# Mixing x before its context in layer 0 of a two-stream block, with the split weights kept in DRAM

## The chip, the cores and the metric

One core of a Trainium2 chip runs one program. Its engines are TensorE (PE, with the load of the stationary operand shown as PEld), VectorE (DVE), ScalarE (ACT), GpSimd (POOL) and SyncE (SP), which issues nearly all DMAs. The metric is the device time of one execution in microseconds. A profile of one execution is shown beside the runs' times; its rows and lines are those of the kernel's source.

## The reference

All tensors are float32. Block 1 has two layers over two streams, x of 512 tokens and a context of 256, both 1024 wide, with the same weights. What concerns the change is the mixer of layer 0, which both streams go through:

```python
for l in range(DEPTH):                       # DEPTH = 2
    h  = modulate(rms_norm(x,  mix_pre_g[l]), sh1,  sc1)
    hc = modulate(rms_norm(xc, mix_pre_g[l]), shc1, scc1)
    p, pc = h @ w_in[l], hc @ w_in[l]        # last layer: only k, v of pc
    # q, k, v; k_all = [kc, k], v_all = [vc, v]
    attn = latent_attention(q, k_all, v_all)
    y = mixer_merge(p, attn, w_attn_o[l], ..., w_gmlp_o[l], ..., w_conv_o[l], w_out[l])
    x = x + g1 * rms_norm(y, mix_post_g[l])
    h2 = modulate(rms_norm(x, ffn_pre_g[l]), sh2, sc2)
    x = x + g2 * rms_norm(square(relu(h2 @ w_ff1[l])) @ w_ff2[l], ffn_post_g[l])
    if not last:                             # the same for the context, on kc, vc alone
        yc = mixer_merge(pc, gqa_attend(qc, kc, vc), ...)
        xc = xc + gc1 * rms_norm(yc, ...)
        xc = xc + gc2 * rms_norm(feed forward of hc2, ...)

def mixer_merge(...):
    a_out = attn @ w_attn_o
    g_out = chunk_spatial_gate(gelu(gu), rms_norm(gelu(gv)), ws, bs) @ w_gmlp_o
    c_out = silu(layer_norm(conv31(a * sigmoid(b)))) @ w_conv_o
    return (ga * a_out + gg * g_out + gc * c_out) @ w_out
```

The context of layer 0 takes keys and values of its own only; those of x take the context's too. A second block of other mixers follows, which the change leaves as it is.

## The kernel before, in words

Activations lie by feature: a tensor of 1024 features is eight tiles of 128 rows, with its tokens along the free axis (`FM`). Every large product is made in three parts. Each operand is given as two float32r parts, hi and lo, whose sum is the float32 value, and `mm3` (L219) multiplies hi by hi, hi by lo and lo by hi. A weight comes in chunks of 128 x 1024 (512 KB), which make one tile of 128 output features; `gemm` (L226) gives 24 products for it, of 256 columns for the context and 512 for x.

`wload` (L195) brings a chunk: a DMA into a tile wr, a cast on ScalarE that gives wh, and a subtraction that gives wl, on VectorE or, if `pool_share` is 2, on GpSimd for every second chunk. There are four slots each of wr, wh and wl. The wr slots are shared with the chunks of `ada_w` (L396), from which background jobs make the modulation vectors.

```python
nc.sync.dma_start(raw, ap)
nc.scalar.copy(hi, raw)
eng.tensor_tensor(lo, raw, hi.bitcast(F32), ALU.subtract)
```

`first_block` (L954) sets the order. In layer 0: four column groups of `ada_w`; the context's norm, K and V; the context's `mixer` (L824) with `pool_share` at 2 and its w_out, beside which x is normed; K and V of x, in two halves of 256 tokens; the `mixer` of x, with the rest of layer 0's `ada_w` beside it and the rest of the context's mixer (`chain_jobs`: residual, norm, feed-forward input) at its end; w_out of x in halves; then the feed-forward `ff` (L859) of both streams.

A mixer has the attention (`attention`, L503), the branch of `w_attn_o`, the spatial gate (`gmlp`), the branch of `w_gmlp_o`, and at the end the branch of `w_conv_o`. Beside the first branches run the 31 taps of the convolution for each of eight tiles (`conv_jobs`, L692, taps at L722), as background jobs spread over about 45 units of products; `conv_act_jobs` then norms the result beside the eight gates of the last branch. 88 chunks of 512 KB are used by each mixer (queries 8, convolution inputs 16, gates 24, three output projections 24, gu 8, gv 8), and w_out has 8 more.

`ff` computes the hidden layer in quarters. The first quarter has two passes over the same eight chunks, back and forth: the context and the first half of x, then the second half of x, since the chain of that half runs beside the first pass.

The framework schedules the whole program: it fixes each engine's order ahead of the run from a timeline that it computes. On each engine, instructions are taken up in that order.

Of the kernel before, what the change touches and what calls it, by code (L numbers as in the profile page):

```python
# [17 lines left out]
P = 128  # L18
D = 1024
# [18 lines left out]
class FM:  # L38
    """A [n * 128, T] tensor kept as tiles of 128 rows, two to a slot if T is 256."""
# [15 lines left out]
class Cols:  # L55
    """Columns c0..c1 of an FM."""
# [20 lines left out]
class Parts:  # L77
    """An FM in parts of 256 tokens that live on their own."""
# [15 lines left out]
def advance(g, n=1):  # L94
    """Up to n steps of a generator; False when it is done."""
    for _ in range(n):
        if next(g, "end") == "end":
            return False
    return True


def interleave(a, b, na, nb):
    """na steps of a, then nb of b, and so on until both are done."""
    la = lb = True
    while la or lb:
        la = la and advance(a, na)
        lb = lb and advance(b, nb)


class Builder:  # L110
    def __init__(self, es, tc, I):
        self.tc, self.nc, self.I = tc, tc.nc, I
        self.uid = 0
        self.wcount = self.pool_share = 0
        ent = es.enter_context
# [32 lines left out]
    def psum2(self, name="s"):  # L148
        """A second set of banks: for chains, or for the scores."""
# [69 lines left out]
    def mm3(self, ps, a, b, start, stop):  # L219
        """ps (+)= a^T b with both given as (hi, lo)."""  # L220
# [5 lines left out]
    def gemm(self, ps, W, act, n=P, ks=range(KT), first=0, last=KT - 1):  # L226
        """ps[n columns of W, T] = W^T act."""
# [4 lines left out]
    def wload_tok(self, ap):  # L232
        """256 columns to be multiplied by token: per k tile the (hi, lo) [128, 256]."""
        r = []
        for u in range(2):
            W = self.wload(ap[u])
# [3 lines left out]
    def gemm_tok(self, ps, W, act, j):  # L240
        """ps[128 tokens, 256] = act[:, tokens j]^T W."""
# [3 lines left out]
    def split(self, src, hi, lo):  # L245
        """hi + lo = src exactly (to 24 bits)."""
# [4 lines left out]
    def colsum(self, acc, T, ps=None):  # L251
        """PSUM [128 tokens, T / 128]: sums of acc over its partitions."""
# [5 lines left out]
    def rsqrt(self, ss, n, scale, post=None, rows=P):  # L258
        """(ss * scale + EPS) ** -0.5 (times post) on [rows, n]."""
# [11 lines left out]
    def bcast(self, col, T, ps=None):  # L271
        """PSUM [128, T]: the column values [128 tokens, T / 128] on every partition."""
# [6 lines left out]
    def add_sq(self, acc, src, k, tile, eng=None):  # L279
        """acc (+)= src ** 2."""  # L280
# [11 lines left out]
    def norm_apply(self, x, T, bc, A, B, hi, lo, ks=range(KT)):  # L292
        """hi + lo = x * bc * A + B, bc by token and A, B by feature."""
# [23 lines left out]

    def load_half(self, x, dram, i):
        """Tokens 256 i and on of a [128, 8 * T] tensor."""
# [128 lines left out]
    def win(self, l, c0):  # L448
        return self.wload(self.I["w_in"][l, c0 // P, 0])
# [1577 lines left out]
```

## Time and profile before

| what | us |
|---|---|
| median of 3 runs | 3567.91 (3563.28 to 3569.14) |
| profiled execution, span from the first to the last instruction (the page tells no other time of it) | 3564.5 |
| PE busy | 3439.1 (96%) |
| DVE busy | 2183.6 (61%) |
| ACT busy | 1512.1 (42%) |
| POOL busy | 981.6 (28%) |
| DMA | 404.82 MB, mean 114 GB/s |

A busy time is the union of an engine's instructions, so a waiting engine is idle, and a product that takes twice as long at the lower granted clock counts as busy for all of it. PEclk is the mean of the clock that was granted in a stretch, as a share of the full one. Products overlap their neighbours in the records, so their pace is told by their count in a stretch, not by the duration of one. Idle time says most where a stage is looked at by itself.

### The profile page before, as it was taken

The page shows a single profiled execution, that of the slowest core. Times are in us where ns is not written, and L with a number is a line of the kernel's source. Part 1 is how long each engine was busy: PE and PEld are TensorE (multiplying, and loading weights), DVE is VectorE, ACT ScalarE, POOL GpSimd, SP SyncE. Part 2 cuts the span into 40 slices and gives each one's busy share as a digit, 9 for nine tenths or more (in the row PEclk, how much of TensorE's full clock was granted, in tenths as well). Part 3 has the DMA queues.
Part 4 walks back from the last instruction along what each step waited for, and adds up shares of the span by engine and source line. Part 5 has one row for each costly group of instructions (what it writes and reads, how often), then busy time and mean ns, then how long its engine had stood idle before and what let it go on. Part 6 is the DMA issues. An engine that isn't in the chain of part 4 may idle for free.

```text
span 3564.5 us, 55040 instructions
## 1 busy us (share of the span) xinstructions
PE 3439.1 (96%) x21553; PEld 3021.4 (85%) x21553; DVE 2183.6 (61%) x3728; ACT 1512.1 (42%) x2594; POOL 981.6 (28%) x987
## 2 busy tenths in 40 slices
PE   7888899999999999999899999999999999999999
PEld 6888889788789888889889898889888987889888
DVE  4789756877956423236756888857233756664334
ACT  4443556333245322225566243246323555544223
POOL 3344423002135300104522012225001436432002
PEclk9899899999999999999999999999999999999999
DMA  6243520333434433334520222334233420044333
GB/s 237 100 154 131 184 95 25 119 131 119 148 112 155 153 114 127 122 107 149 165 71 19 95 95 84 100 124 152 91 101 119 132 87 27 1 152 132 95 100 120
DMA packets 133220, 404.82 MB, mean 114 GB/s; under 512 B 13664, under 2 KB 38624, under 8 KB 132832
## 3 DMA queue, kind: packets, MB, share of 16 engines
q1 hardware_dynamic: 132960, 401.30, 34.3%
q8 instruction: 170, 2.79, 0.3%
q14 instruction: 90, 0.74, 0.1%
HBM read 386.56 MB, written 14.68 MB: 113 GB/s over the span
## 4 chain that ended last, share of the span: by engine, by line
PE 84%; DVE 7%; ACT 3%; issue 1%; POOL 1%; DMA 0%; POOLq 0%; ACTq 0%; DVEq 0%
PE f L222 12%; PE f L224 12%; PE f L223 12%; DVE yc L722 3%; PE pg L222 3%; PE pg L223 3%; PE pg L224 3%; PE pb L222 2%; PE pb L224 2%; PE pb L223 2%; PE c L222 2%; PE c L224 2%; PE c L223 2%; DVE wl L205 2%; PE ada L400 1%
## 5 line engine op out<-in xcount | busy, mean ns | idle before, releaser
L202 ACT CAST wh<-wr 128x1024 fp32r<-128x1024 f32 x586 | 613.1, 1049 | 1377.9 <-PE f L223 496.0
L205 DVE TENSOR_TENSOR wl<-wr,wh 128x1024 fp32r<-128x1024 f32 (+1 forms) x542 | 716.6, 1323 | 532.6 <-ACT wh L202 523.8
L887 POOL TENSOR_TENSOR relu<-relu 128x256 f32<-128x256 f32 (+1 forms) x154 | 141.4, 920 | 911.2 <-ACT hxh L886 619.8
L722 DVE SCALAR_TENSOR_TENSOR yx<-gl,pcol,yx 128x512 f32<-128x512 f32 x480 | 367.4, 769 | 10.3
L222 PE MATMUL f<-hx2h,wh 128*128 128x512 f32 (+1 forms) x648 | 224.7, 352 | 1.4 <-ACT hx2h L303 1.3
L222 PE MATMUL f<-hxh,wh 128*128 128x512 f32 x576 | 226.0, 394 | 0.0
L224 PE MATMUL f<-hx2h,wl 128*128 128x512 f32 (+1 forms) x648 | 223.9, 347 | 0.0
L223 PE MATMUL f<-hx2l,wh 128*128 128x512 f32 (+1 forms) x648 | 223.7, 347 | 0.0
L224 PE MATMUL f<-hxh,wl 128*128 128x512 f32 x576 | 223.7, 389 | 0.0
L223 PE MATMUL f<-hxl,wh 128*128 128x512 f32 x576 | 223.6, 389 | 0.0
L905 DVE TENSOR_TENSOR fyx<-f,fyx 128x256 f32<-128x256 f32 x144 | 56.0, 419 | 173.9 <-PE f L224 173.9
L264 POOL TENSOR_TENSOR sm<-sm,mhalf 128x2 f32<-128x2 f32 (+4 forms) x91 | 94.2, 1038 | 188.4 <-DVE sm L262 183.8
L722 DVE SCALAR_TENSOR_TENSOR yc<-gl,pcol,yc 128x256 f32<-128x256 f32 x240 | 144.4, 652 | 0.6
L222 PEld LDWEIGHTS f<-hx2h,wh 128*128 128x128 f32 x648 | 122.6, 192 | 23.7 <-issue 4.1
L224 PEld LDWEIGHTS f<-hx2h,wl 128*128 128x128 f32 x648 | 123.8, 191 | 16.1 <-DVE mod L417 0.4
L223 PEld LDWEIGHTS f<-hx2l,wh 128*128 128x128 f32 x648 | 123.6, 191 | 14.6 <-DVE hx2l L305 0.4
L205 POOL TENSOR_TENSOR wl<-wr,wh 128x1024 fp32r<-128x1024 f32 x44 | 113.3, 2576 | 82.2 <-ACT wh L202 82.2
L222 PEld LDWEIGHTS f<-hxh,wh 128*128 128x128 f32 x576 | 108.1, 188 | 28.6 <-issue 5.8
L224 PEld LDWEIGHTS f<-hxh,wl 128*128 128x128 f32 x576 | 108.1, 188 | 22.8
L223 PEld LDWEIGHTS f<-hxl,wh 128*128 128x128 f32 x576 | 108.2, 188 | 21.7
L890 DVE TENSOR_TENSOR hxl<-relu,hxh 128x256 fp32r<-128x256 f32 (+1 forms) x98 | 57.8, 592 | 106.3 <-POOL relu L887 106.3
L551 POOL TENSOR_SCALAR p<-p,sm 128x768 f32<-128x768 f32 (+1 forms) x80 | 65.9, 824 | 200.5 <-DVE sm L550 161.3
(665 smaller groups left out, 10758.6 us busy)
## 6 DMA issues: line engine op xcount, KB each, us to landing
wr<-in_w_ff_dram SPq DMA_DIRECT2D x234, 512.0 KB, 3.5
wr<-in_w_in_dram SPq DMA_DIRECT2D x199, 512.0 KB, 3.5
wr<-in_ada_w_dram SPq DMA_DIRECT2D x96, 512.0 KB, 3.7
wr<-in_w_out_dram SPq DMA_DIRECT2D x44, 512.0 KB, 4.3
wr<-in_w_in_t_dram SPq DMA_DIRECT2D x36, 512.0 KB, 3.9
wr<-in_w_attn_o_dram SPq DMA_DIRECT2D x24, 512.0 KB, 3.5
wr<-in_w_gmlp_o_dram SPq DMA_DIRECT2D x24, 512.0 KB, 3.5
wr<-in_w_conv_o_dram SPq DMA_DIRECT2D x24, 512.0 KB, 3.5
```

The lines of the kernel that those rows point to most:

```text
L202: nc.scalar.copy(hi, raw)
L205: eng.tensor_tensor(lo, raw, hi.bitcast(F32), ALU.subtract)
L222: mm(ps, a[0], b[0], start=start, stop=False)
L223: mm(ps, a[0], b[1], start=False, stop=False)
L224: mm(ps, a[1], b[0], start=False, stop=stop)
L264: nc.gpsimd.tensor_tensor(r, v, self.mhalf[0:rows].to_broadcast([rows, n]), ALU.pow)
L400: nc.tensor.matmul(v[c][r], self.st[:, 2 * g + u, :], raw[:, (2 * u + h) * CW:(2 * u + h + 1) * CW], start=(g == 0), stop=(g == 3))
L551: nc.gpsimd.tensor_scalar(p[:, :W], p[:, :W], rc, 1.0, op0=ALU.mult, op1=ALU.mult)
L722: nc.vector.scalar_tensor_tensor(Y.k(k), src, w, Y.k(k), op0=ALU.mult, op1=ALU.add)
L887: nc.gpsimd.tensor_tensor(r, r, r, ALU.mult)
L890: nc.vector.tensor_tensor(lo.k(k)[:, o], r[:, a - c0:b - c0], hi.k(k)[:, o].bitcast(F32), ALU.subtract)
L905: nc.vector.tensor_add(y.k(k), p, y.k(k))
```

## The change

In layer 0, the norms, K and V of both streams come first (`kv` now takes x as a whole, one load of its weights for all 512 tokens). The context's h, K and V are stored in DRAM (`put_away`), and their tiles come free. Then the mixer of x runs; with `wmode` at "store", `wload` also stores wh and wl of each chunk. After w_out of x the mode is "load": the context's h, K and V come back, its mixer runs, and each of its 96 chunks (w_out included) is two DMAs straight into wh and wl, or into two wr tiles for every third chunk. There is no cast and no subtraction for them, and `pool_share` stays 0. The jobs of the chain of x's second half run beside the context's attention (`beside`), those of the context's chain beside the first pass of the feed-forward, which is now x as a whole, then the context. The context's y is no longer stored. K and V of layer 1 are made as before.

```diff
-    def wload(self, ap, n=KT * P):
+    def wload(self, ap, n=KT * P, key=None):
         nc = self.nc
+        if key and self.wmode == "load":
+            self.wcount += 1
+            r = []
+            for u, tag in enumerate(("wr", "wr") if self.wcount % 3 == 0 else ("wh", "wl")):
+                w = self.wp.tile([P, KT * P], F32R, tag=tag, bufs=NB[tag], name=self.nm(tag))[:, 0:n]
+                nc.sync.dma_start(w.bitcast(F32), self.wd[key][u][:, 0:n])
+                r.append(w)
+            return r
...
+        if key and self.wmode == "store" and key not in self.wd:
+            self.wd[key] = [self.dp.tile([P, KT * P], F32, name=self.nm("wd")) for _ in range(2)]
+            for w, d in zip((hi, lo), self.wd[key]):
+                nc.sync.dma_start(d[:, 0:n], w.bitcast(F32))
         return hi, lo
+    def put_away(self, x):
+        d = {}
+        for i, t in x.tiles.items():
+            d[i] = self.dp.tile([P, S], F32, name=self.nm("away"))
+            self.nc.sync.dma_start(d[i], t.bitcast(F32))
+        def back(n=x.n, T=x.T, name=x.name):
...
-        for n, (c0, c1) in enumerate(HALVES):
+        for n, (si, c0, c1) in enumerate([(0, *c) for c in HALVES] if extra else [(0, 0, S), (1, 0, NCTX)]):
             for k, W in load(n):
-                for si in range(1, len(sts)):
-                    if not n:
-                        up(k, W, si, 0, sts[si].T)
-                up(k, W, 0, c0, c1)
+                up(k, W, si, c0, c1)
...
-        ci = self.load_x(I["ctxT"], NCTX, "ci")
+        ci, xi = self.load_x(I["ctxT"], NCTX, "ci"), self.load_x(I["xT"], S, "xi")
...
         stats(1, ci, NCTX)
+        stats(0, xi, S)
...
-                kvc = self.kv(sc, l, h[1], 0, NCTX)
-                self.pool_share = 2
...
-                mg = self.mixer(sc, l, h[1], [kvc], jobs=more)
...
-                kvs = [self.kv(sx, l, h[0], *c) for c in HALVES] + [kvc]
+                self.norm_apply(xi, S, self.bcast(rs[0], S), A[0], B[0], *h[0])
+                del ci, xi
+                kvc, = self.kv(l, [(sc, h[1], 0, NCTX)])
+                away = [self.put_away(x) for x in h.pop(1) + kvc[0] + kvc[1]]
+                kvs = self.kv(l, [(sx, h[0], 0, S)]) + [kvc]
+                self.wmode = "store"
...
+            if not last:
+                self.wmode = "load"
+                sts.append(sc)
+                away = [f() for f in away]
+                h[1], kvc = away[0:2], (away[2:4], away[4:6])
+                del away
+                self.bg = []
+                mg = self.mixer(sc, l, h[1], [kvc], beside=list(pre))
...
+                pre = self.chain_jobs(y, NCTX, lambda acc=acc: acc, G1[1], x, A2[1], B2[1], h2[1],
+                                      lambda x=x: self.store_x(x, dram["c1"]))
```

The order of SP in the mixer of x, at the first gates after the attention. wr are loads of chunks (in_w_in, in_ada_w); wd are the stored parts. Before:

```order
L199 DMA wr_7177<-in_w_in_dram 128x1024
L396 DMA wr_7216<-in_ada_w_dram 128x1024
L199 DMA wr_7223<-in_w_in_dram 128x1024
L396 DMA wr_7260<-in_ada_w_dram 128x1024
L199 DMA wr_7268<-in_w_in_dram 128x1024
```

and in the changed kernel:

```order
L219 DMA wd_2987<-wh_2983 128x1024
L219 DMA wd_2988<-wl_2984 128x1024
L209 DMA wr_3080<-in_w_in_dram 128x1024
L219 DMA wd_3037<-wh_3033 128x1024
L219 DMA wd_3038<-wl_3034 128x1024
L425 DMA wr_3120<-in_ada_w_dram 128x1024
L219 DMA wd_3086<-wh_3082 128x1024
L219 DMA wd_3087<-wl_3083 128x1024
L209 DMA wr_3129<-in_w_in_dram 128x1024
```

Between two loads of w_in there now stand two or four stores, each of which waits for the part that it stores.

The order of SP at the begin of the context's mixer, changed kernel (hch, hcl, kch and so on are the context's h, K and V in two parts; away their places in DRAM; wd stored weights):

```order
L205 DMA wh_7813<-wd_1072 128x1024
L205 DMA wl_7815<-wd_1073 128x1024
L205 DMA wh_7871<-wd_1148 128x1024
L205 DMA wl_7873<-wd_1149 128x1024
L343 DMA hch_1599_7611<-away_641 128x512
L343 DMA hch_1600_7613<-away_643 128x512
L343 DMA hch_1601_7615<-away_645 128x512
L343 DMA hch_1602_7617<-away_647 128x512
L343 DMA hcl_1603_7619<-away_649 128x512
```

The reload of the context's h stands behind the fourth pair that goes into wh and wl; that pair takes the slots of the last chunk of x's w_out.

## Rows read from the trace of the kernel before

**Rows 1.** The page, shares of the chain that ended last, by engine.
```profile
PE 84%; DVE 7%; ACT 3%; issue 1%; POOL 1%; DMA 0%; POOLq 0%; ACTq 0%; DVEq 0%
```
**Rows 2.** Busy time by stage; x is the number of instructions, us from the start.
```profile
core 0: us, PE busy (x) PEld busy (x) DVE busy (x) ACT busy (x) POOL busy (x), PEclk, DMA share, GB/s
0.00:56.00 56.00, 34.55 (x242) 20.44 (x243) 19.86 (x66) 16.12 (x27) 12.37 (x20) 0.85 0.81 281
56.00:124.00 68.00, 61.86 (x452) 57.74 (x451) 40.60 (x96) 45.02 (x97) 34.51 (x34) 0.89 0.36 117
124.00:338.00 214.00, 190.81 (x1476) 187.06 (x1477) 196.78 (x307) 91.62 (x138) 93.55 (x59) 0.95 0.41 138
338.00:438.00 100.00, 82.73 (x607) 80.25 (x607) 84.02 (x121) 53.17 (x90) 49.05 (x34) 0.88 0.52 170
438.00:463.00 25.00, 25.00 (x212) 25.00 (x211) 15.51 (x28) 16.52 (x30) 5.68 (x8) 1.00 0.57 184
463.00:650.00 187.00, 180.95 (x1200) 162.66 (x1199) 117.61 (x224) 114.58 (x201) 48.23 (x48) 1.00 0.14 45
650.00:1091.00 441.00, 440.69 (x2312) 358.32 (x2311) 343.29 (x487) 151.31 (x222) 80.59 (x67) 1.00 0.40 132
1091.00:1141.00 50.00, 48.47 (x399) 47.78 (x398) 30.17 (x49) 30.48 (x61) 26.76 (x30) 1.00 0.57 188
1141.00:1224.00 83.00, 81.49 (x662) 74.90 (x660) 48.30 (x94) 38.80 (x82) 39.81 (x51) 0.98 0.40 129
1224.00:3565.00 2341.00, 2292.51 (x14008) 2007.30 (x14007) 1287.50 (x2261) 954.51 (x1650) 591.02 (x640) 0.99 0.32 104
```
**Rows 3.** The same view, only the context's w_out (woc); the columns are PE, PEld, ACT.
```profile
414.60:437.80 23.20, 23.20 (x192) 23.02 (x192) 2.55 (x7) 1.00 0.69 231
```
**Rows 4.** Groups by line, 124 to 338: busy us, mean ns, idle before.
```profile
L722 DVE SCALAR_TENSOR_TENSOR yc<-gl,pcol,yc 128x256 f32<-128x256 f32 x216 | 130.7, 657 | 0.3
L205 DVE TENSOR_TENSOR wl<-wr,wh 128x1024 fp32r<-128x1024 f32 x29 | 48.5, 1674 | 9.3 <-ACT wh L202 9.2
...
L205 POOL TENSOR_TENSOR wl<-wr,wh 128x1024 fp32r<-128x1024 f32 x29 | 75.3, 2599 | 59.8 <-ACT wh L202 59.8
```
**Rows 5.** Groups of DVE, 205 to 209, where GpSimd makes no wl.
```profile
L722 DVE SCALAR_TENSOR_TENSOR yc<-gl,pcol,yc 128x256 f32<-128x256 f32 x9 | 3.7, 472 | 0.0
```
**Rows 6.** Waits of PE, 56 to 438: us in total, times, longest.
```profile
PE pb L224 <- DVE wl L205: 8.9, 8, 2.0
PE c L224 <- DVE wl L205: 7.6, 3, 3.8
```
**Rows 7.** Busy time, a stretch of queued loads and one of the mixer of x.
```profile
14.00:22.00 8.00, 4.17 (x28) 2.15 (x32) 4.22 (x16) 2.23 (x7) 0.71 (x1) 1.00 1.03 410
...
650.00:800.00 150.00, 150.00 (x851) 122.05 (x850) 121.52 (x175) 43.59 (x67) 0.63 (x8) 1.00 0.42 142
```
**Rows 8.** DMA issues of the run: count, KB each, median us to landing.
```profile
xn<-x SPq DMA_DIRECT2D x16, 256.0 KB, 5.0
```
**Rows 9.** Timeline of POOL, the last tiles of the context's norm: start us, us.
```profile
47.35 2.51 POOL L304 TENSOR_SCALAR f<-u,A,B 128x256 f32<-128x256 f32 x3 [0.15 <-POOL f L304]
```
**Rows 10.** Groups of POOL, 385 to 438, the norm of x.
```profile
L304 POOL TENSOR_SCALAR f<-u,A,B 128x512 f32<-128x512 f32 x8 | 15.5, 1944 | 4.6 <-ACT hxh L303 3.5 <-DVE u L297 1.0
```
**Rows 11.** Busy time in a stretch of the feed-forward with 512 columns alone.
```profile
2600.00:2650.00 50.00, 50.00 (x222) 41.44 (x221) 17.69 (x22) 16.12 (x22) 5.20 (x5) 1.00 0.29 95
```
**Rows 12.** Busy time at the begin of layer 0's feed-forward.
```profile
1141.00:1160.00 19.00, 17.49 (x134) 17.20 (x133) 12.77 (x27) 10.91 (x22) 11.57 (x16) 0.91 0.27 83
```

More of the change, by code (lines that the diff above doesn't have):

```diff
@@ L114, in __init__ @@
         self.wcount = self.pool_share = 0
+        self.wmode, self.wd = None, {}
         ent = es.enter_context
@@ L316, in load_x @@
         return x
+    def put_away(self, x):
[4 more added lines that the diff above has]
+        def back(n=x.n, T=x.T, name=x.name):
+            y = FM(self, n, T, F32R, name)
+            for i, a in d.items():
+                y.k(i * y.per)
+                self.nc.sync.dma_start(y.tiles[i].bitcast(F32), a)
+            return y
+        return back
     def load_half(self, x, dram, i):
@@ L465, in rope, with kv @@
         return a
[L467 to L470 removed]
+    def kv(self, l, parts):
+        nc = self.nc
         g = self.pcol[l][:, PC_KN:PC_KN + 1]
[L472 to L496 removed]
@@ new lines, in kv @@
+        r, pend = [], []
+        hv = [[Cols(x, c0, c1) for x in h] for _, h, c0, c1 in parts]
+        for i, (st, h, c0, c1) in enumerate(parts):
+            T = c1 - c0
+            r.append([(self.new_act(256, "k" + st.name, 2), self.new_act(256, "v" + st.name, 2))
+                      for _ in range(T // 256)])
+        Wk = [None, None]
+        for m in range(2):
+            Wk[m] = self.win(l, K0 + m * P)
+            for i, (st, h, c0, c1) in enumerate(parts):
+                T = c1 - c0
+                ps = self.psum("k")[:, :T]
+                self.gemm(ps, Wk[m], hv[i])
+                sq = self.n("ksq", T)
+                nc.scalar.activation(sq, ps, AF.Square)
+                if st.ctx:
+                    a = self.n("ka", T)
+                    nc.scalar.activation(a, ps, AF.Copy, scale=g)
+                else:
+                    a = self.rope(ps, T, c0, g)
+                pend.append((i, m, T, a, sq))
+                self.tick()
@@ new lines, in kv @@
+        W = self.win_tok(l, V0)
+        ss = None
+        for i, (st, h, c0, c1) in enumerate(parts):
+            for j in range((c1 - c0) // P):
+                ps = self.psum("v")[:, :CW]
+                self.gemm_tok(ps, W, hv[i], j)
+                V = r[i][j // 2][1]
+                self.split(ps, V[0].k(j % 2), V[1].k(j % 2))
+                if ss is None:
+                    ss = [self.colsum(sq, T) for _, _, T, _, sq in pend]
+                    rs = [self.rsqrt(x, p[2] // P, 1.0 / P) for x, p in zip(ss, pend)]
+                self.tick()
@@ L497, in kv, with attention @@
+        for x, (i, m, T, a, sq) in zip(rs, pend):
+            bc = self.bcast(x, T)
             nc.vector.tensor_mul(a, a, bc)
-            self.split(a, K[0].k(m), K[1].k(m))
-        return K, V
-    def attention(self, st, l, h, kvs, fill=()):
+            for u, (K, _) in enumerate(r[i]):
+                self.split(a[:, u * 256:u * 256 + 256], K[0].k(m), K[1].k(m))
+        return [kv for x in r for kv in x]
+    def attention(self, st, l, h, kvs, fill=(), beside=()):
         nc, T, nqp = self.nc, st.T, st.nt // 2
@@ L604, in attention @@
                 fill.pop(0)()
+            if beside:
+                beside.pop(0)()
+        for j in beside:
+            j()
         return O
@@ L822, in spread, with mixer @@
         self.bg_rate = len(self.bg) / units + 1e-6 if units else 1.0
-    def mixer(self, st, l, h, kvs, early=(), jobs=lambda: ()):
+    def mixer(self, st, l, h, kvs, early=(), jobs=lambda: (), beside=()):
         nc, T = self.nc, st.T
@@ L831, in mixer @@
             fill, conv = conv[:2], conv[2:]
-            O = self.attention(st, l, h, kvs, fill)
+            O = self.attention(st, l, h, kvs, fill, beside)
             n = len(conv) // (len(early) + 1)
@@ L1015, in context @@
                 late["G2"] = [self.fold(l, s, 5, PC_FFPOST, False, "G2") for s in range(2)]
-                if last:
-                    return ()
-                y, x = self.load_x(dram["yc"], NCTX, "yc"), self.load_x(I["ctxT"], NCTX, "xc")
-                acc = self.acc(NCTX, "cacc")
-                for k in range(KT):
-                    self.add_sq(acc, y.k(k), k, self.n)
-                h2.append(self.new_act(NCTX, "hc2"))
-                sts.append(sc)
-                return self.chain_jobs(y, NCTX, lambda: acc, late["G1"][1], x, late["A2"][1], late["B2"][1],
-                                       h2[0], lambda: self.store_x(x, dram["c1"]))
-            mg = self.mixer(sx, l, h[0], kvs, self.ada_jobs(0, 4, 12) if not last else (), context)
+                return ()
+            mg = self.mixer(sx, l, h[0], kvs, self.ada_jobs(0, 4, 12) if not last else (), folds)
+            h.pop(0)
             G1, A2, B2, G2 = (late[n] for n in ("G1", "A2", "B2", "G2"))
@@ L1031, in first_block @@
             pre = []
-            load = self.keeping(lambda k: self.wload(I["w_out"][l, k, 0]))
+            load = self.keeping(lambda k: self.wload(I["w_out"][l, k, 0], key=("w_out", l, k)))
             for i, (c0, c1) in enumerate(HALVES):
```

78 lines of the change are left out of this document (22 added, 56 removed).

## Prediction

> **What bounds the kernel now.** I read the page's chain first, then the busy time by stage, then inside the two stages that the change touches. The chain of the whole run is 84% TensorE [rows 1], so a stage gains only what keeps TensorE waiting or running slowly in it. The stages [rows 2] tell where that is. In the mixer of x (463 to 1091) and in the feed-forward, PE is busy in nearly every microsecond at a granted clock of 1.00 or 0.99. In the context's mixer (56 to 438, with its w_out) it is not: clock 0.89, 0.95 and 0.88, and PE busy 61.9 of 68, 190.8 of 214 and 82.7 of 100 us, so 46.6 us idle.
>
> What would that stage take with no wait? Its w_out stretch runs unhindered: 192 products of 256 columns in 23.20 us, 120.8 ns each [rows 3]. The stage has 452 + 1476 + 607 = 2535 products [rows 2], 306 us at that pace. It takes 382. The excess of 76 us is 13.4, 35.7 and 26.7 us in its three rows; beyond the idle time it is products at the lower of the clock's two levels.
>
> The middle row's cause is VectorE: 196.8 of 214 us busy. Of this 130.7 us are 216 taps of the convolution at 657 ns, and 48.5 us are 29 low parts of weights, while GpSimd makes 29 more at 2599 ns [rows 4]. A tap takes only 472 ns where GpSimd makes no low part [rows 5]. PE's largest waits in this stage name the same line, the subtraction that makes wl [rows 6]. So splitting a weight for only 256 tokens costs more vector time than PE needs to use it.
>
> **The change, part by part.** *The context's mixer.* It loses all splits: 96 chunks. The 248 taps then cost 248 x 0.472 = 117 us, and even with the other VectorE work of the middle row (196.8 - 130.7 - 48.5 = 18 us) VectorE is far below the 178 us (1476 x 0.1208) of PE there. What replaces the splits is a second DMA for each chunk. 96 pairs of 1.049 MB are 100.7 MB; the twelve reloaded tiles and ctxT make it 104.8 MB. While loads stand in a queue the trace shows 410 GB/s (14 to 22 us) [rows 7]: 256 us, below PE's 306. From a mean share and rate, 138 GB/s at 0.41 [rows 2], a full share would be 337 GB/s: 311 us, about PE's own. Six slots of pairs let loads queue, so I take a rate near 410.
>
> Against this speaks the Trainium skill, HBM Reference, Specifications (TRN2): a core has a share of about 358 GB/s when both cores of a pair stream, and alone measures about 425. By 358 a pair would take 2.93 us against 24 x 0.1208 = 2.90 of PE, and the sum would be some 7 us worse, w_out of x included. The 410 of this trace, with one core at work, is nearer to the other figure.
>
> Now the three rows. First: 54.6 us of products keep their excess of 13.4, since the chain from scores to values stays as it was and x's second chain now runs beside it. Added is the reload of the context's h, K and V, which the order puts behind the fourth pair of weights, and that pair waits for the last chunk of x's w_out. One pair and 2.1 MB of h at 410 GB/s are 7.7 us; one landing of a loaded 256 KB tile, 5.0 us [rows 8], is the least and 12.7 us (both in a row) the most; I take 8. So 76 us. Second: 178.3 us, with 6 of the 35.7 us excess left (ends 0 and 35.7, near the low end as its cause is removed), so 184. Third: 73.3 us, with 5 of 26.7 left, since eight gates (23 us) cover the norm's chain once the taps are not late. So 78. Sum 338 against 382: **-44 us**, with ends 306 (no stall) and 381 (rival B).
>
> *The mixer of x.* Each of 88 chunks now also leaves by two stores. In 650 to 1091 the kernel moved 441 us x 132 GB/s = 58 MB [rows 2]; 78 stored pairs add 82, 140 MB in all, which needs 318 GB/s. At 410 that is 342 us and hidden; at 337, 416 us and still hidden. In 650 to 800, with 142 GB/s before [rows 7], it is about 332. On SP a store waits for the low part, but the next load into that slot waits for the same low part, so the issues behind it lose little. A slot of wh is held longer, until its store lands. Ends 0 and +58 (rival A); I take **+5**.
>
> *w_out of x.* Its first pass moves 8 x 1.573 = 12.6 MB in 8 x 2.90 = 23 us; at 410 GB/s that is 31 us. The second pass loads only four chunks and makes up for most. Ends 0 and +7.5; I take **+2**.
>
> *The start.* x (2.1 MB) is now loaded among the first ada chunks, where the DMA engines are full: 5.1 us. Its norm is no longer hidden by the context's w_out. GpSimd ends the context's eight tiles at 49.9 us [rows 9]; then come x's eight at 1944 ns, 15.5 us [rows 10]. 49.9 + 5.1 + 15.5 is 70.5; then about 1 us for the last low part, 1.4 us for the last products of K and 96 products of V, 11.6 us. So x's queries start at about 84.5 us. Before, this work ended after 56 us and 25 us (438 to 463) [rows 2], together 81: **+4**, with ends 0 and +12.
>
> *The feed-forward.* Its first pass takes x whole: 192 products of 512 columns, 222 in 50 us [rows 11], so 225 ns each and 43.2 us, for 384 of 256, 46.4 us. That is -3.2. The stage's begin (1141 to 1160) has 134 products, 16.2 us, in 19 us [rows 12]; it waited for the chain of x's second half, which now runs beside the context's attention: -2.8. The context's chain hides behind the 43 us. Together **-6**. The chain's own instructions are as many as before: 0, their cover being x's 43 us of products; without it they would cost the 2.8 us that I take off.
>
> Sum: -44 + 5 + 2 + 4 - 6 = -39 against the span of 3564.5 us, so 3525.5. The median of the runs shown, 3567.9, lies 3.4 us above that span, which I add: **3529 us**.
>
> **The rivals.** *A: the stores choke the mixer of x, and the kernel gets slower.* If loads and stores together get only 281 GB/s, the mean of the first 56 us [rows 2], where loads of several sizes mix, the 140 MB take 499 us in place of 441: +58 in place of +5. That gives 3564.5 - 39 - 5 + 58 + 3.4 = 3582. It costs from 318 GB/s down, and decides the sign from about 287 down. For it: VectorE is busy 343 of 441 us there [rows 2], so a late load also holds taps up. Against it: the 410 GB/s.
>
> *B: the context's mixer becomes bound by DMA.* At the same 281 GB/s its 104.8 MB take 373 us, with the start's 8 us 381: nothing is gained, 3572. It begins below 310 GB/s. Against it: nothing but loads runs there, in rows as long as those of the 410.
>
> *C: nearly all waits go.* 312 us for the context, nothing lost at the start or to stores: 3564.5 - 70 + 2 - 6 + 3.4 = 3494. Against it: the reload stall is in the order.
>
> That the change does not do what it says can be excluded from the order: the context's loads read the stored parts.
>
> **How the numbers follow.** A measurement tells 0.2% (7 us) from no change. Forecast 0.64, its own range 3497 to 3556; A 0.14; B 0.10; C 0.12. Faster: 0.64, C, and half of B (rates between 281 and 310): 0.81. Same: the rest of B and 0.03 of A: 0.08. Slower: 0.11. The range goes from just below C to A: 3487 to 3582.
>
> **What would show it.** Right: no split of the 96 chunks in the context's mixer, taps near 472 ns, that stage near 338 us at a DMA rate over 300 GB/s, the mixer of x still with PE busy throughout from its attention on. Wrong: PE's waits in the context's mixer name DMAs of wh, wl or wr throughout, not only at its start; PE idle in the mixer of x with waits for splits that waited for loads or for slots held by stores; x's queries starting after 95 us.

## The result and the profile after

| | before | after |
|---|---|---|
| median of 4 runs each, us | 3567.16 (3563.28 to 3569.14) | 3525.81 (3525.37 to 3527.21) |
| ratio, 95% interval | | 0.9884 (0.9870 to 0.9898) |
| span of the profiled execution, us | 3564.5 | 3525.4 |

The changed kernel is 41 us faster (1.2%); 3529 was predicted. The page's chain (shares by engine) has moved to TensorE, from 84% [rows 1] to

```profile
PE 91%; ACT 3%; DVE 2%; DMA 2%; POOL 1%; issue 1%; SPq 0%; POOLq 0%; ACTq 0%; DVEq 0%
```

The busy time by stage of the changed kernel, which answers to [rows 2]; the bounds are the first products of each stage. In order: the start; the attention of x; the rest of the mixer of x; its w_out; the wait for the context's reload; the context's attention; the rest of its mixer with the taps; its last gates; its w_out; the feed-forward's begin; the rest.

```profile
core 0: us, PE busy (x) PEld busy (x) DVE busy (x) ACT busy (x) POOL busy (x), PEclk, DMA share, GB/s
0.00:97.10 97.10, 65.17 (x431) 47.86 (x431) 48.08 (x114) 40.04 (x66) 31.39 (x34) 0.89 0.75 266
97.10:284.00 186.90, 180.83 (x1192) 162.90 (x1190) 117.42 (x224) 116.19 (x203) 48.28 (x48) 0.99 0.35 125
284.00:724.20 440.20, 440.20 (x2310) 358.76 (x2309) 337.29 (x472) 147.29 (x208) 63.85 (x59) 1.00 0.83 304
724.20:771.50 47.30, 47.30 (x395) 47.11 (x393) 21.63 (x30) 22.70 (x48) 19.99 (x22) 1.00 0.91 328
771.50:780.50 9.00, 1.79 (x10) 1.07 (x9) 6.55 (x18) 5.26 (x10) 7.26 (x11) 0.76 1.04 406
780.50:850.00 69.50, 62.40 (x449) 59.26 (x450) 35.12 (x116) 37.26 (x94) 24.27 (x39) 0.88 0.60 225
850.00:1029.00 179.00, 177.59 (x1482) 177.39 (x1483) 130.09 (x306) 32.98 (x78) 18.61 (x31) 1.00 0.93 345
1029.00:1076.10 47.10, 47.10 (x396) 47.10 (x395) 17.77 (x47) 20.41 (x43) 6.58 (x9) 1.00 0.97 353
1076.10:1099.30 23.20, 23.20 (x194) 23.19 (x194) 1.89 (x3) 7.84 (x18) 5.16 (x7) 1.00 0.69 249
1099.30:1182.60 83.30, 83.30 (x504) 68.35 (x503) 44.08 (x73) 35.00 (x63) 28.55 (x33) 1.00 0.52 171
1182.60:3525.40 2342.80, 2290.71 (x13969) 2004.65 (x13968) 1286.84 (x2254) 953.59 (x1647) 591.64 (x639) 0.99 0.32 103
```

Two things are to be seen. From 850 to 1099 us the context's mixer now runs with PE busy in 247.9 of 249.3 us at the full clock, where before the same work took 312.9 us (124.9 to 437.8, by the first gate's product). And the start, 97.1 us, is longer than the two stretches that it replaces (56.0 and 25).

Put together by the first products of each stage (or the last of the stage before it) in the two profiles, in us:

| part | before | after | difference | predicted |
|---|---|---|---|---|
| start, to x's first query | 81.2 | 97.1 | +15.9 | +4 |
| mixer of x | 628.4 | 627.1 | -1.3 | +5 |
| w_out of x | 49.4 | 47.3 | -2.1 | +2 |
| context's mixer and w_out | 381.8 | 327.8 | -54.0 | -44 |
| feed-forward of layer 0 | 586.3 | 578.4 | -7.9 | -6 |
| layer 1 | 1070.6 | 1072.2 | +1.6 | 0 |
| second block to its last w_out | 360.8 | 369.6 | +8.8 | 0 |
| end | 406.0 | 405.9 | -0.1 | 0 |
| sum | 3564.5 | 3525.4 | -39.1 | -39 |

The sum came out almost as predicted, but three of its rows did not: the start, the context and the second block. The experiments look into these.

First, the groups of the changed kernel on VectorE between 850 and 1064 us (busy us, mean ns, idle before). The 29 splits of [rows 4] are gone, and a tap takes 498 ns where it took 657 there and 472 in [rows 5]:

```profile
L767 DVE SCALAR_TENSOR_TENSOR yc<-gl,pcol,yc 128x256 f32<-128x256 f32 x240 | 109.0, 498 | 3.1
L678 DVE TENSOR_TENSOR sg<-pb,sg 128x256 f32<-128x256 f32 x11 | 4.7, 423 | 6.0 <-PE pb L238 5.7 <-issue 0.2
```

And PE's waits in the whole stage of the context, 771.5 to 1099.3 us (us in total, times, longest), the first four:

```profile
PE q L236 <- DMA hch<-away: 3.6, 1, 3.6
PE bc L289 <- POOL sm L278: 2.2, 1, 2.2
PE sc L236 <- DVE sm L586: 2.0, 1, 2.0
PE q L237 <- DMA hcl<-away: 1.9, 1, 1.9
```

The waits for wl of [rows 6] are no longer among them. The only waits for a DMA are the two for the reload of the context's h, at the stage's begin.

### The profile page after: what moved, and what is told of

It is laid out like the page before. It is cut to its first block, busy times and chain, and to the rows that moved or that the text cites. A ratio compares the mean times of both kernels' runs of the same rounds, so it can differ in the third digit from the quotient of the medians.

```text
span 3525.4 us, 54772 instructions
## 1 busy us (share of the span) xinstructions
PE 3419.6 (97%) x21313; PEld 2997.6 (85%) x21313; DVE 2046.7 (58%) x3652; ACT 1418.6 (40%) x2472; POOL 845.6 (24%) x931
## 4 chain that ended last, share of the span: by engine, by line
PE 91%; ACT 3%; DVE 2%; DMA 2%; POOL 1%; issue 1%; SPq 0%; POOLq 0%; ACTq 0%; DVEq 0%
PE f L236 12%; PE f L238 12%; PE f L237 12%; PE pg L236 3%; PE pb L236 3%; PE pg L237 3%; PE pg L238 3%; PE pb L238 3%; PE pb L237 3%; PE c L236 2%; PE c L238 2%; PE c L237 2%; PE ada L429 1%; PE wo L236 1%; PE wo L237 1%; PE wo L238 1%
## 5 line engine op out<-in xcount | busy, mean ns | idle before, releaser
L212 ACT CAST wh<-wr 128x1024 fp32r<-128x1024 f32 (+1 forms) x486 | 508.8, 1049 | 1240.4 <-PE f L237 500.7
L215 DVE TENSOR_TENSOR wl<-wr,wh 128x1024 fp32r<-128x1024 f32 (+1 forms) x486 | 629.3, 1296 | 538.5 <-ACT wh L212 530.3
L767 DVE SCALAR_TENSOR_TENSOR yx<-gl,pcol,yx 128x512 f32<-128x512 f32 x480 | 368.0, 770 | 10.3
L932 POOL TENSOR_TENSOR relu<-relu 128x512 f32<-128x512 f32 (+1 forms) x146 | 137.9, 946 | 904.3 <-ACT hxh L931 592.7
L237 PE MATMUL f<-hx2l,wh 128*128 128x512 f32 (+1 forms) x584 | 211.9, 364 | 0.0
L236 PEld LDWEIGHTS f<-hx2h,wh 128*128 128x128 f32 x584 | 110.2, 190 | 23.2 <-issue 2.1
L238 PEld LDWEIGHTS f<-hx2h,wl 128*128 128x128 f32 x584 | 110.8, 190 | 17.5
L237 PEld LDWEIGHTS f<-hx2l,wh 128*128 128x128 f32 x584 | 110.7, 190 | 16.5
L935 DVE TENSOR_TENSOR hxl<-relu,hxh 128x512 fp32r<-128x512 f32 (+1 forms) x90 | 55.3, 616 | 101.5 <-POOL relu L932 101.5
L679 POOL TENSOR_TENSOR mx<-mx,sg 128x512 f32<-128x512 f32 x32 | 50.9, 1591 | 263.8 <-DVE sg L678 263.8
L236 PE MATMUL f<-h4h,wh 128*128 128x512 f32 (+1 forms) x328 | 112.5, 343 | 0.0
```

Source lines behind the costliest of these rows:

```text
L236: mm(ps, a[0], b[0], start=start, stop=False)
L237: mm(ps, a[0], b[1], start=False, stop=False)
L238: mm(ps, a[1], b[0], start=False, stop=stop)
L679: nc.gpsimd.tensor_tensor(merged.k(k), merged.k(k), sg.k(k), ALU.add)
L767: nc.vector.scalar_tensor_tensor(Y.k(k), src, w, Y.k(k), op0=ALU.mult, op1=ALU.add)
L932: nc.gpsimd.tensor_tensor(r, r, r, ALU.mult)
```

## The experiments

All but one start from the changed kernel. The kernel before ran beside them, and ratios are against those runs; its median was 3568.73 us beside the first four runs told here (stores, loads, splits), 3569.27 beside those with x's norm moved, the reload issued early and both of these, and 3568.76 beside the two with keys and values in one call.

No edit touches what lies behind the context's w_out. It takes 2426.1 and 2426.7 us in the two profiles of the changed kernel, and 2420.6 to 2424.2 in the profiles of the ten kernels with edits. So 2 to 6 us by which a run below is shorter than the changed kernel need not come from its edit. What an edit does is read from the stages ahead of that point.

### Do the stores cost anything: one pair stored, all loads from it

```diff
-            self.wd[key] = [self.dp.tile([P, KT * P], F32, name=self.nm("wd")) for _ in range(2)]
-            for w, d in zip((hi, lo), self.wd[key]):
-                nc.sync.dma_start(d[:, 0:n], w.bitcast(F32))
+            if not self.wd:
+                self.wd[0] = ...
+                ...
+            self.wd[key] = self.wd[0]
```

> One chunk is stored and every load of the context's mixer reads that one place, so the mixer of x runs without its 174 other stores and the context multiplies by a wrong weight; all instructions of the compute engines are as in the changed kernel. Theory (the stores are hidden behind TensorE): the mixer of x with w_out, 97 to 772 us in the changed kernel, stays within 4 us of its 674 us, and the run within 6 us of 3526. Rival A (the stores cost, and the removal of the context's chain from the mixer of x hides that): that stage becomes 10 us or more shorter, the run under 3516.

Measured: 3527.37 us, ratio 0.9884 (0.9870 to 0.9899), the same as with 96 stored pairs. The rows of this kernel from x's first query to the end of its w_out (the same three stretches as above):

```profile
98.40:285.40 187.00, 180.93 (x1199) 162.68 (x1197) 118.71 (x226) 116.11 (x203) 48.41 (x48) 1.00 0.14 46
285.40:724.80 439.40, 439.40 (x2303) 357.49 (x2302) 336.71 (x470) 146.67 (x208) 66.67 (x59) 1.00 0.39 127
724.80:772.10 47.30, 47.30 (x395) 47.11 (x393) 21.13 (x30) 22.90 (x48) 18.35 (x21) 1.00 0.63 207
```

The three stretches take 673.7 us against 674.4 with the stores, though the DMA rate falls from 304 to 127 GB/s in the second and from 328 to 207 in the third. PE is busy throughout in these two, with the stores and without. So the stores, 88 pairs and w_out's 8, are hidden: my +5 and +2 were not there to be paid.

### How near is rival A: every part stored twice

```diff
             for w, d in zip((hi, lo), self.wd[key]):
                 nc.sync.dma_start(d[:, 0:n], w.bitcast(F32))
+            for w in (hi, lo):
+                d = self.dp.tile([P, KT * P], F32, name=self.nm("wd2"))
+                nc.sync.dma_start(d[:, 0:n], w.bitcast(F32))
```

> Each part is stored twice, to two places. 650 to 1091 us of the kernel before would move 58 + 164 MB, 222 MB, in the 441 us that TensorE needs: 503 GB/s. Theory (stores are hidden only as long as loads and stores together stay under about 410 GB/s): it no longer fits; 222 MB at 410 GB/s are 541 us, so the mixer of x becomes some 100 us longer (60 to 140), the run 3585 to 3665, and TensorE waits there. If stores had a path of their own, beside the loads: less than 20 us.

Measured: 3646.11 us, ratio 1.0215 (1.0200 to 1.0230). Rows of the mixer of x and its w_out:

```profile
284.00:400.00 116.00, 106.79 (x507) 81.33 (x506) 87.95 (x128) 21.36 (x24) 0.48 (x6) 0.99 1.00 388
400.00:817.50 417.50, 362.11 (x1804) 291.88 (x1803) 240.08 (x341) 122.71 (x181) 68.86 (x53) 0.93 0.99 383
817.50:894.50 77.00, 57.83 (x397) 54.60 (x396) 29.87 (x49) 29.73 (x58) 26.73 (x30) 0.87 1.01 392
```

and PE's largest waits between 96.9 and 894.5 us:

```profile
PE pb L241 <- DVE wl L215: 19.2, 12, 3.2
PE pg L241 <- DVE wl L215: 13.8, 6, 4.3
PE wo L239 <- ACT wh L212: 10.6, 5, 3.1
```

So this is what a choked mixer looks like: the DMA share at 0.99 to 1.01 for 610 us, the clock down to 0.93 and 0.87, and PE waiting for splits, whose casts on ScalarE wait 101.6 us in all for loads into wr. From x's first query to the end of w_out it takes 797.6 us (96.9 to 894.5) in place of 674.4, inside the 60 to 140 us more that were expected. The rate at full share is 383 to 392 GB/s, loads and stores together. The three rows carry 235.1 MB (45.0, 159.9 and 30.2); in the changed kernel its rows from 284.0 to 771.5 carry 149.3 MB (133.8 and 15.5), which at 388 GB/s need 385 us of the 487.5 that PE needs. Rival A's mechanism is real, but the change stands about a fifth away from it.

### Is the context's mixer bound by DMA: one load for each chunk

```diff
-            for u, tag in enumerate(("wr", "wr") if self.wcount % 3 == 0 else ("wh", "wl")):
-                w = ...
-                nc.sync.dma_start(w.bitcast(F32), self.wd[key][u][:, 0:n])
-                r.append(w)
-            return r
+            tag = "wr" if self.wcount % 3 == 0 else "wh"
+            w = ...
+            nc.sync.dma_start(w.bitcast(F32), self.wd[key][0][:, 0:n])
+            return [w, w]
```

> Each chunk of the context's mixer is one load in place of two; the hi part serves as both, so the low part is wrong. Theory (TensorE paces the context's mixer, the DMA engines keep up at 340 to 356 GB/s): 850 to 1099 us of the changed kernel, 249 us, stays within 4 us; only the stall at the begin of the context's mixer (9 us before its first product) becomes shorter, by some 2 to 4 us. Rival B (it is at the limit of the DMA engines): that stretch becomes 10 us or more shorter, since half the bytes are gone.

Measured: 3519.11 us, ratio 0.9862 (0.9847 to 0.9876). Its three rows of the context: the wait for the reload, the attention, the rest with w_out.

```profile
771.40:776.40 5.00, 1.36 (x9) 1.03 (x9) 3.34 (x10) 3.19 (x7) 3.99 (x7) 0.94 0.80 262
776.40:845.80 69.40, 62.44 (x451) 59.34 (x450) 38.37 (x124) 39.34 (x98) 27.62 (x44) 0.88 0.42 141
845.80:1094.00 248.20, 247.82 (x2067) 247.62 (x2067) 153.94 (x359) 60.13 (x138) 32.88 (x47) 1.00 0.54 179
```

With half the traffic (179 GB/s in place of 345 to 353) the long row is 248.2 us against 249.3: the stored parts arrive in time, and rival B is out. Only the first row shortens, from 9.0 to 5.0 us; the reload has less ahead of it in the queue. The attention stays at 69.4 us, so its excess over the bare pace does not come from DMAs.

### What the order does by itself: the new order with the old splits

```diff
-                self.wmode = "store"
...
-                self.wmode = "load"
+                self.pool_share = 2
...
-                self.wmode = None
+                self.pool_share = 0
```

> The new order of the changed kernel, but nothing of the weights is stored or loaded back: the context's mixer splits its 96 chunks again, every second one on GpSimd as in the kernel before. Theory (the splits on VectorE and GpSimd are what held the context's mixer): its stage goes from 328 us back to 370 to 385, the run to 3565 to 3585, no faster than the kernel before. Rival (the new order gave the gain): the stage stays under 345 us and the run under 3545.

Measured: 3602.74 us, ratio 1.0095 (1.0078 to 1.0112), slower than the kernel before, by more than expected. Its rows of the context, the same stretches as in the changed kernel (the wait, the attention, the part with the taps, w_conv_o with w_out), then the taps and the low parts on both engines from 867 to 1126 us:

```profile
771.80:781.70 9.90, 2.62 (x13) 2.06 (x13) 4.45 (x12) 4.07 (x8) 9.28 (x12) 0.72 0.69 233
781.70:867.10 85.40, 69.33 (x452) 65.78 (x451) 53.97 (x130) 49.99 (x110) 43.80 (x50) 0.79 0.34 114
867.10:1125.80 258.70, 217.16 (x1683) 212.29 (x1682) 236.48 (x363) 107.35 (x165) 109.94 (x67) 0.94 0.41 139
1125.80:1179.40 53.60, 49.79 (x385) 48.55 (x386) 29.07 (x36) 29.84 (x54) 30.24 (x20) 0.95 0.49 158
```
```profile
L767 DVE SCALAR_TENSOR_TENSOR yc<-gl,pcol,yc 128x256 f32<-128x256 f32 x240 | 147.4, 664 | 0.6
L215 DVE TENSOR_TENSOR wl<-wr,wh 128x1024 fp32r<-128x1024 f32 x34 | 57.3, 1687 | 7.5 <-ACT wh L212 7.5
```
```profile
L215 POOL TENSOR_TENSOR wl<-wr,wh 128x1024 fp32r<-128x1024 f32 x34 | 87.3, 2570 | 77.1 <-ACT wh L212 77.1
```

VectorE is full again (236.5 of 258.7 us) and a tap back at 664 ns. The stage takes 407.6 us against 381.8 before and 327.8 with the stored parts, so the gain comes from the stored parts and not from the order. The order with the old splits costs 34 us (3602.7 against 3568.7): the start (x's queries at 97.1 here too, +15.9) and the context's begin, where the wait and the attention take 95.3 us against 68.9 before (56.0 to 124.9). The other stages of layer 0 give 11 us of it back, 7.8 of them in the feed-forward, and what lies behind layer 0 takes 5.9 us more. The part behind the attention takes 312.3 us, as before (312.9). The stored parts then give 77 us (3602.7 to 3525.8); by the rows, 63 us behind the attention (312.3 to 249.3) and 17 in it and the wait (95.3 to 78.5). The two can't be told apart fully: with the stored parts the context's begin is only 9.6 us longer than before, with the splits 26.4, and the old order with stored parts was not run.

### The start: x's norm behind the context's keys, whole or half

```diff
-                self.norm_apply(xi, S, self.bcast(rs[0], S), A[0], B[0], *h[0])
-                del ci, xi
+                del ci
                 kvc, = self.kv(l, [(sc, h[1], 0, NCTX)])
                 away = ...
+                self.norm_apply(xi, S, self.bcast(rs[0], S), A[0], B[0], *h[0])
+                del xi
```

Here it is the whole norm; in the second run tiles 0 to 3 stay ahead of `kv` and tiles 4 to 7 follow it. What they test stands in the trace of the changed kernel. PE's longest wait there between 40 and 97.1 us:

```profile
PE cs L269 <- ACT ksq L514: 9.4, 1, 9.4
```

cs is the column sum over the squares of the context's keys, 4 products of one column, and in PE's fixed order it stands ahead of all of x's keys. The timeline of ACT (start us, us) says why its square came late: it was put behind the tiles of x's norm.

```profile
67.38 0.81 ACT L317 ACTIVATE hxh<-u,B,A 128x512 fp32r<-128x512 f32 x1 [0.39 <-DVE u L311]
68.10 0.36 ACT L514 ACTIVATE ksq<-k 128x256 f32<-128x256 f32 x1
```

So PE stood still while ScalarE made the last five of x's eight tiles (59.5 to 68.2 us); then came all 48 products, partly at a granted clock below 1.00, and the 96 of the values (the three stretches of the changed kernel):

```profile
58.90:68.50 9.60, 0.18 (x2) 0.00 (x0) 9.13 (x13) 5.81 (x9) 8.87 (x5) 0.70 0.70 222
68.50:83.20 14.70, 14.69 (x62) 12.20 (x63) 6.20 (x12) 6.02 (x13) 2.96 (x4) 0.85 0.37 133
83.20:97.10 13.90, 13.90 (x121) 13.90 (x120) 4.90 (x9) 6.04 (x11) 3.21 (x3) 1.00 0.45 169
```

> The norm of x is emitted after the context's K and V instead of before them, so that ScalarE takes the squares of the context's K before the eight tiles of x. Theory (the 16 us that the start lost come from the colsum of the context's K at the head of TensorE's queue, which waited 9.4 us for a square that stood behind the whole norm of x on ScalarE): that wait goes; x's norm then starts only at about 60 us, so x's queries start at 88 to 92 us instead of 97, run 5 to 9 us shorter. Rival (the norm itself, 15.5 us on GpSimd, sets the start): x's queries at 95 us or later, run unchanged.

Measured: 3523.51 us, ratio 0.9872 (0.9857 to 0.9887); x's queries start at 92.7 us, just outside the theory's 88 to 92, and the run is 2.3 us shorter than the changed kernel, not 5 to 9. The wait for ksq is gone, but PE now waits for tiles of the two norms (its two largest waits between 40 and 92.7 us in this run):

```profile
PE k L236 <- ACT hch L317: 3.7, 1, 3.7
PE k L236 <- ACT hxh L317: 2.4, 1, 2.4
```

> As e1_norm_late, but only tiles 4 to 7 of x's norm are emitted after the context's K and V, tiles 0 to 3 before. Theory: the squares wait for four tiles only, TensorE has the products of these tiles to go on with, and x's queries start at 82 to 87 us; run 10 to 15 us shorter than the changed kernel. Rival (the norm itself sets the start): no better than 95 us.

Measured: 3518.44 us, ratio 0.9862 (0.9847 to 0.9876); the queries at 92.0 us, which misses what was expected. The run is 7.4 us shorter than the changed kernel, but the context's w_out ends only 4.7 us earlier. The wait for ksq shrinks from 9.4 to 2.2 us, but the second half of x's norm now stands behind work for the context's keys (its last hxh at 75.1 us, not 67.4), and x's keys follow it.

### The start again: keys and values of both streams in one call

```diff
-                kvc, = self.kv(l, [(sc, h[1], 0, NCTX)])
+                kvc, *kvs = self.kv(l, [(sc, h[1], 0, NCTX), (sx, h[0], 0, S)])
                 away = [self.put_away(x) for x in h.pop(1) + kvc[0] + kvc[1]]
-                kvs = self.kv(l, [(sx, h[0], 0, S)]) + [kvc]
+                kvs += [kvc]
```

> Only the start is changed: the keys and values of the context and of x are made by one call, so that their weights are loaded and split once, the context's keys stand between those of x in PE's queue, and the column sums over the squared keys stand behind the first values of both, where their squares have long been made. Theory (the head of PE's queue was the larger part of the start's excess, and x's keys can end with the last tile of x's norm): PE's wait for ksq of 9.4 us is gone, x's last product of the keys is at 70 to 74 us, then 48 and 96 products of values (17 us): x's queries at 87 to 91 us against 97.1, and the run 6 to 10 us shorter than the changed kernel (3516 to 3520). Rival (the norm of x and the lower clock set the start by themselves): the queries at 94 to 98, the run within 3 us of the changed kernel's.

Measured: 3517.82 us, ratio 0.9857 (0.9841 to 0.9873), 8 us below the changed kernel (4.7 us of it by the end of the context's w_out); queries at 92.2 us, between the theory's 87 to 91 and the rival's 94 to 98. PE's waits between 40 and 92.2 us no longer name ksq; the largest is

```profile
PE k L237 <- DVE hcl L319: 3.5, 4, 1.1
```

The last product of x's keys ends at 71.8 us, inside what the theory gave, against 83.2 in the changed kernel. So the queue's head was what kept x's keys from following the norm. The values took 20.5 us to the queries, not 17: 24 column sums stand among the 144 products, and six more short products (bc) behind them.

```profile
71.70:92.20 20.50, 20.50 (x176) 20.50 (x174) 8.40 (x16) 10.20 (x20) 6.93 (x6) 1.00 0.50 180
```

Of the 12.6 us by which the start missed its forecast (97.1 against 84.5) this run wins 4.9 back, the two others 4.4 and 5.1 in their own ways; the earliest queries of any run were at 89.8 us. Where an edit leaves the start alone they came at 96.9 to 99.5. In this run the rest does not lie in the norm, as the rival had it. The keys end 1.1 us before the 72.9 that the forecast needed (84.5 less 11.6 for the values); the rest lies in the products between the keys and the queries, where the context's 48 now stand too, with PE busy throughout at the full clock.

### The reload issued ahead of w_out of x

```diff
             h.pop(0)
+            if not last:
+                away = [f() for f in away]
             G1, A2, B2, G2 = ...
...
                 sts.append(sc)
-                away = [f() for f in away]
```

> The reload of the context's h, K and V is emitted ahead of w_out of x, so that it stands before the context's weights on SyncE. Theory (the 9 us between the last product of x's w_out and the context's first are the landing of this reload behind the fourth pair): the gap shrinks to under 3 us, run 6 to 9 us shorter. Rival (w_out of x then lacks slots for tiles and is held up itself, or the weights land late instead): less than 3 us shorter, or longer.

Measured: 3523.40 us, ratio 0.9875 (0.9859 to 0.9892). The gap is gone (w_out of x ends at 773.4, the context's first query starts at 773.3 us), as the theory had it, but the run gains 2.4 us (3525.81 to 3523.40), the rival's number. W_out of x takes 48.4 us in place of 47.3, the attention 73.5 in place of 69.5, and the part behind it 251.9 in place of 249.3; x's first query came at 99.5 us in this profile, 2.4 later. Nor was the gap empty: in its 9.0 us DVE worked 6.55 us, ACT 5.26 and POOL 7.26, and the row of the attention here has about as much more of their work:

```profile
773.30:846.80 73.50, 64.19 (x459) 60.82 (x458) 41.28 (x133) 42.84 (x104) 32.69 (x50) 0.88 0.62 233
```

That fits the longer attention, but does not show that it is the cause.

### Both together

> e8_norm_halves and e6_early_back together. If both theories hold their gains add: 16 to 24 us shorter than the changed kernel, 3502 to 3510 us.

Its edit is that of the norm in halves and that of the early reload. Measured: 3515.58 us, ratio 0.9854 (0.9839 to 0.9868). The gains add (7.4 and 2.4 us apart, 10.2 together), but each is smaller than its theory had it, so 3502 to 3510 is missed.

> The same with the reload of h, K and V issued ahead of w_out of x. Theory (both gains add): the queries at 87 to 91 us, no idle time of PE between w_out of x and the context's queries (9.0 us before), run 3513 to 3518. Rival (they don't add, as the attention behind gives the gap back): within 2 us of the run with the keys and values together alone.

Keys and values in one call, with the early reload. Measured: 3509.16 us, ratio 0.9833 (0.9818 to 0.9848): the fastest version, 17 us below the changed kernel (by its median of 3525.81) and below the 3513 to 3518 expected. By the end of the context's w_out it is 13.4 us ahead (1085.9 against 1099.3). Both gains are in the rows, the start at 90.4 us and no idle stretch between w_out of x and the context's attention (71.9 us, with nothing ahead of it):

```profile
0.00:90.40 90.40, 65.18 (x425) 47.57 (x425) 42.01 (x106) 36.09 (x60) 28.91 (x34) 0.89 0.71 256
718.10:766.50 48.40, 47.56 (x396) 47.31 (x395) 22.28 (x30) 22.73 (x48) 20.26 (x22) 1.00 1.00 368
766.50:838.40 71.90, 61.86 (x459) 58.89 (x458) 40.92 (x133) 42.92 (x104) 32.87 (x50) 0.93 0.63 237
```

The early reload is worth 8.7 us here (3517.82 to 3509.16), where it gave 2.4 on the changed kernel and 2.9 with the norm in halves (3518.44 to 3515.58). Why it pays in full only beside keys and values in one call was not settled.

### Both kernels profiled again: the second block

Without an edit.

> The kernel before, profiled a second time. Between the two first profiles the second block (from its first product at 2797.7 us before, 2749.9 after, to its last w_out at 3158.5 and 3119.5) took 360.8 us before and 369.6 after, though the change leaves it as it is; in the profiles of the experiments it took 365 to 367. Theory: that difference is one execution against another, so this profile shows 364 to 370 us there. Rival: the change slows the second block itself (another order, another clock), and this profile shows 359 to 362 again.

> The changed kernel, profiled a second time. Theory (one execution against another): the second block takes 364 to 368 us here, and the two kernels' second profiles differ by less than 3 us in it; the stages of layer 0 are within 2 us of the first profile (x's queries at 97, the context's stage 328 us). Rival (the change slows the second block): 369 to 371 again.

Measured: 3570.58 us before and 3528.08 after. The second block to its last w_out, of the kernel before in its first and in its second profile:

```profile
2797.70:3158.50 360.80, 338.92 (x2492) 289.42 (x2492) 242.83 (x661) 189.25 (x401) 159.86 (x208) 0.98 0.16 54
```
```profile
2798.80:3162.90 364.10, 343.14 (x2493) 292.57 (x2493) 242.23 (x660) 189.17 (x401) 159.34 (x207) 0.97 0.16 53
```

and of the changed kernel in its second:

```profile
2750.90:3120.40 369.50, 343.83 (x2493) 292.52 (x2493) 245.91 (x660) 189.31 (x401) 160.53 (x208) 0.96 0.16 53
```

The first number lies at the low end of what one execution against another would give (364), the second in the rival's range. Before varies by 3.3 us (360.8 and 364.1), so that much of the 8.8 us can be one execution against another; but 5.4 us stay between the second profiles, where less than 3 were expected. The work is the same (2493 products), and the granted clock is a little lower each time (0.98, 0.97, 0.96). In the ten runs with edits the block took 365.2 to 367.1 us, less than in either profile of the changed kernel. Why the clock falls in other places there after the change was not settled. The stages of layer 0 repeat: in the second profiles the start is 81.3 and 97.6 us and the context's stage 381.4 and 327.6.

## Why the prediction held, and where it did not

**Context's mixer, -44, measured -54.** The mechanism was as predicted: the splits gone, taps at 498 ns (472 forecast), a DMA rate of 345 to 353 GB/s where over 300 was asked, one wait for the reload, which I took at 8 us and which took 9.0. By rows, the first was 78.5 us (76 forecast), the other two 249.3 where I had 184 + 78 = 262. I had left 6 and 5 us of the old excess in them; nothing was left: 2072 products in 249.3 us are 120.3 ns each, the pace of [rows 3]. The term was sized too small by that remainder.

**Mixer of x, +5, measured -1.3; w_out of x, +2, measured -2.1.** The stores are hidden: without them the stretch is as long. The 140 MB that I gave 650 to 1091 were 133.8 MB in 440.2 us. The rate that I leaned on, 410 GB/s of [rows 7], was too high for long stretches (383 to 392 with loads and stores); the 8 us before that stretch (6 to 14 us) had shown 347 at a share of 1.01. But PE needs only 304. The other rate that I named, 337, was too low. Against the Trainium skill (HBM Reference, Specifications (TRN2)), which gives a core about 358 GB/s when its pair streams too and about 425 alone, the 383 to 392 of the run with doubled stores lie between; this measurement decides. By the Trainium skill's 358 the 149.3 MB would need, as an estimate, 417 us and be hidden as well.

**Start, +4, measured +15.9: the step that failed.** I wrote that after the last tile of x's norm come "1.4 us for the last products of K", as if x's keys could follow the tiles as they came. The order had the answer: PE's queue held the context's column sums ahead of x's keys, and ACT's held their squares behind x's tiles. So all 48 products came after: 13.8 us (69.4 to 83.2), 12.4 more than I took. With that head out of the way they ended at 71.8 us. The values took 13.9 against 11.6 (121 products stand there, not 96), the norm ended 2 us earlier than I said; 12.4 + 2.3 - 2.1 are the 12.6 us missing. I had named a start after 95 us as a sign of a wrong step, and it was one.

**Feed-forward, -6, measured -7.9.** The begin runs with PE busy in 83.30 of 83.30 us and clock 1.00, where the row before had 81.49 of 83.00 at 0.98 [rows 2]. Of the 7.9 us, 7.1 lie ahead of the first product of the second projection (83.9 us before, 76.8 after), where both terms were expected; the two, -3.2 and -2.8, were not told apart.

**Rest, 0, measured +10.3** (layer 1 +1.6, second block +8.8, end -0.1). The kernel before varied by 3.3 us in the second block from one profile to the other, so that much can be one execution against another; the rest is open. The total was right partly by luck: the start's missing 11.9 and these 10.3 us offset the context's extra 10.0, the 10.4 of the mixer of x and its w_out, and the 1.9 of the feed-forward. The 3.4 us that I added for the median were too much as well: the median of after lies 0.4 us above the span of its profile.

**The rivals.** A needs more than the change stores: with doubled stores it cost 123 us in its stage, and the 235.1 MB of its rows fill their 610.5 us at 385 GB/s. B is excluded by the run with one load for each chunk. C's number (312 us for the context) was missed by 15.8 us, all in the attention and the reload: behind them nearly all waits did go. The outcome lies in the forecast's own range of 3497 to 3556.

## What to carry to other kernels

Splitting or converting a weight twice can cost more than writing the result out once and reading it back, if the stage that stores has DMA capacity to spare and the stage that loads has vector work that the conversion slows: count the bytes of each stage against a rate seen over a long stretch, and the vector time against TensorE's bare pace. A reordering has a price of its own (34 us here, with the old splits), which a gain elsewhere can hide: measure it with the new order and the old work. And where an order is fixed ahead, look at what stands at the head of a queue between two independent pieces of work; four products of one column kept TensorE idle for 9.4 us, since their input was made late on another engine.

## What the runs showed of the hardware

One core's loads and stores of 512 KB together held 383 to 392 GB/s for 610 us at a DMA share of 0.99 to 1.01, while loads alone showed 410 over 8 us [rows 7].

The taps measure what GpSimd's subtractions cost VectorE: 664 ns on average with them and 498 without, on the same order of work, so 240 taps took 147.4 us of VectorE in place of 109.0. Their shortest, median and longest durations in ns, with the splits and without:

```profile
L767 DVE SCALAR_TENSOR_TENSOR yc<-gl,pcol,yc x240: 467/473/2701, 870.4 to 1101.9; 128x256 f32<-128x256 f32 x120
L767 DVE SCALAR_TENSOR_TENSOR yc<-gl,pcol,yc x240: 471/484/966, 853.4 to 1024.7; 128x256 f32<-128x256 f32 x120
```

The median is no higher with the splits; a few long taps make the mean. Of the 240 with the splits, 201 overlap no subtraction of GpSimd and take 481 ns on average; the 39 that overlap one take 1610, and 19 of them over 2 us. One of these, and the subtraction beside it (start us, us):

```profile
918.01 2.63 DVE L767 SCALAR_TENSOR_TENSOR yc<-gl,pcol,yc 128x256 f32<-128x256 f32 x1
917.14 3.23 POOL L215 TENSOR_TENSOR wl<-wr,wh 128x1024 fp32r<-128x1024 f32 x1
```

This tap ends 0.27 us after the subtraction. The Trainium skill (SBUF — State Buffer, SBUF: two separate sides) says that an operation of VectorE with two inputs from SBUF and one of GpSimd that reads SBUF take turns at a pair of ports, each for a whole instruction. The trace agrees: the longest tap, 2701 ns, is about as long as a whole subtraction (2570 ns on average).
